# Latent attention: one run of value products per unit, with the denominators and the turned maxima inside it, and nine buffers of probabilities

## The chip, the core and the metric

The program runs on one core of one Trainium2 chip. The metric is the device time of one execution in microseconds (us); the time of a kernel is the median of its runs. A profile is one further execution, recorded instruction by instruction by the hardware profiler; its span is counted from the program's first recorded instruction to its last, so the execution's own time is a little longer than the span.

The engines are named as the profile names them: PE multiplies matrices (PEld is its weight load, which overlaps it), DVE works on vectors and can read the accumulator banks of PE (PSUM), ACT evaluates functions and copies, POOL works on vectors in SBUF, SP issues most DMA transfers. Each engine takes its instructions in order.

## The reference

Two layers over 256 context tokens and 1,024 latent tokens of width 1,024: a windowed attention layer, then a latent attention layer, each with modulation, gate and residual, and a final norm. Only the second layer's attention is touched. Cut to that:

```python
qn, qr, kn, kr, v, g = project(h)        # 16 heads; 64 + 32 columns of q and k, 64 of v
s = (einsum("bqhd,bkhd->bhqk", qn, kn)
     + einsum("bqhd,bkd->bhqk", qr, kr)) * scale
p = softmax(s, axis=-1)                  # over 256 + 1024 keys
o = einsum("bhqk,bkhd->bqhd", p, v)
y = (o * silu(g)) @ w_out
```

All is float32, and results are needed for the 1,024 latent queries alone.

## The kernel before

Latent attention is cut into 16 units (class `UnitB`, list `units`). A unit is one pair of heads and one half (512) of the queries; unit `ui` has pair `ui // 2` and half `ui % 2`. Its keys are ten chunks of 128 (`NT = 10`). The order of every instruction in this stage is the order in which the program writes it down (`manual_schedule`), and each engine works through its own part of that order. `u` is the unit at work, `pu` the one before, `nu` and `nnu` the next two.

**Scores.** `score(c, i0, i1)` multiplies the terms `i0` to `i1` of chunk `c`: five terms, each with one matmul per head of the pair (64 rows of the array each, line 1344), into a pair of PSUM banks. Pairs (3, 4) and (5, 6) alternate with `c % 2`; the last unit uses three pairs. After the fifth term ACT takes the exponential of both banks into one of six probability buffers `Er` (line 1348), and POOL adds the buffer to the running sum `acc` from which the denominators come (lines 1352 and 1354; on DVE in the last unit).

**Maxima of the next unit.** An upper bound for the row maximum is found a unit ahead: `nu.top(PIECES[c])` multiplies one piece of `nu`'s queries with keys into two of the banks 0, 1, 2 (line 1310), and DVE reduces each bank (lines 1316 and 1318). `CUT[c]` says after how many terms of chunk `c` this piece stands: 4, 1, 1, 2, 2, 3, 3, 4, 4, 5. At the unit's end `nu.turn` reduces the parts (line 1321) and turns the maxima with four matmuls (line 1324); `nu.shift` writes them with DVE into the rows of `nu.q` that the fifth score term reads (line 1328). So the fifth term of `nu`'s first chunk waits for the shift.

**Values.** `PV(c0, c1)` multiplies chunks of probabilities with the values into bank 7 (line 1361; each float32 product shows as two matmul instructions, so a chunk is four). There are two runs per unit: `PV(0, 5)` ahead of the scores of chunk 5, and `PV(5, NT)` after the last chunk. `fin` copies bank 7 out with ACT (line 1365) and loads the gate rows.

**Denominators.** Ahead of the first run stands `pu.fin2`: four matmuls with ones sum `pu`'s `acc` over its partitions (line 1372), ACT copies them into the first half of `acc` (line 1374). DVE inverts the two halves: `inv(0)` after the first run's place, `inv(1)` at the unit's end between `turn` and `shift` (line 1378). `gate` multiplies `pu`'s output by gate and inverse on POOL (line 1383) and stores it; it stands at chunk 0 of the unit after (`units[ui - 2].gate()`).

**Between units.** After the shift some units hold extra work ("fill"): units 0, 2, 4, 6, 8, 10 and 12 compute the keys of the next pair (`make_K`, three blocks, each copied out by ACT and DVE), units 3, 7 and 11 the values of the next four heads (`make_V`, five blocks, copied out by ACT). Units 1, 5, 9, 13 and 14 have none. Fill uses banks 0, 1, 2 as `top` does. `nnu.prep()` loads the queries of the unit after next into the buffer that the present unit's scores have just been reading, so it can only be issued when the last score is done, and `nu.top` of the next unit reads it first. One piece of the output weights is loaded and split per unit (`wo_fill`, an ACT copy and a POOL subtraction).

The arena `F` (52 KB per partition) holds the probability buffers from 10 KB on, the values from 34, the two `acc` from 44.

Of the kernel before, what the change touches and what calls it, by code (L numbers as in the profile page):

```python
# [22 lines left out]
NT = TOK // 128  # L23
# [1 line left out]
EPS = 1e-6  # L25
KB = 256
R_KB = 152
F_KB = 52
NEG = -1e30
A_SCALE = 64 ** -0.5  # L30
B_SCALE = 96 ** -0.5
# [2 lines left out]
class Ring:  # L34
# [6 lines left out]
    def next(self):  # L41
        b = self.bufs[self.i % len(self.bufs)]
        self.i += 1
        return b


def shp(ap, *dims):
    n = 1
    for d in dims:
        n *= d  # L50
    ap = ap[:, 0:n]
    if len(dims) == 1:
        return ap
    names = "abcdefg"[: len(dims)]
    kw = {c: d for c, d in zip(names[1:], dims[1:])}
    return ap.rearrange("p (" + " ".join(names) + ") -> p " + " ".join(names), **kw)
# [3 lines left out]
def kernel(ctx: ExitStack, tc: tile.TileContext, t, out, dbg=None):  # L60
    nc = tc.nc
# [4 lines left out]
    PB = ppool.tile([128, 8, 512], F32, name="PB")  # L66
    R = cpool.tile([128, R_KB * KB], F32R, name="arena_r")
    F = cpool.tile([128, F_KB * KB], F32, name="arena_f")
    ident = cpool.tile([128, 128], F32, name="ident")
# [16 lines left out]
    def r_at(kb, *dims):  # L86
        n = int(np.prod(dims))
        return shp(R[:, int(kb * KB) : int(kb * KB) + n], *dims)

    def f_at(kb, *dims):  # L90
        n = int(np.prod(dims))
        return shp(F[:, int(kb * KB) : int(kb * KB) + n], *dims)
# [395 lines left out]
    class UnitA:  # L488
# [29 lines left out]
        def score(self, h, later=False):  # L518
            g, qT = self.g, self.qT
            P = Pr.next()  # L520
            q = qT[:, h % 2, h // 2]
            self.Ps.append(P)
            sk = nsink[:, 4 * g + h : 4 * g + h + 1]
            nl = self.nloc * 128
            parts = [(nl, 256, 0, 0)]
            if nl:
                parts.append((0, nl, self.k0 * 128, (self.k0 - (self.ti - 1)) * 128))
            mx = None
            nm = self.nm[:, h : h + 1]
            for i, (po, n, ko, mo) in enumerate(parts):  # L530
                S = pss3()[:, 0:n]
                nc.tensor.matmul(S, q[:, 0], kT[:, g, ko : ko + n], start=True, stop=False)  # L532
                nc.tensor.matmul(S, q[:, 1], kT[:, g, ko : ko + n], start=False, stop=True)  # L533
                prev = sk if mx is None else mx
                mx = nm if i == len(parts) - 1 else self.mx[:, h : h + 1]
                o, mk = P[:, po : po + n], mask[:, mo : mo + n]
                if i == 0:
                    mk = zeros
                nc.vector.tensor_tensor_reduce(o, S, mk, -A_SCALE, prev, ALU.add, ALU.min, mx)  # L539
            if not later:  # L540
                self.exp(h)

        def exp(self, h):
            P, nm = self.Ps[h][:, 0 : self.nk], self.nm[:, h : h + 1]
            nc.scalar.activation(P, P, AF.Exp, bias=nm, scale=-1.0, accum_out=self.den[:, h : h + 1])  # L545
# [40 lines left out]
        def fin2(self, fast=False):  # L586
            g, og = self.g, self.og
            o, o2 = self.o, self.o2
            rt = shp(pst3(), 4, 128)
            for j in range(2):  # L590
                nc.tensor.transpose(rt[:, j, :], self.rb[:, j * 128 : j * 128 + 128], ident)
            rs = shp(rtr.next(), 2, 128)
            eng = nc.vector if fast else nc.gpsimd
            eng.tensor_add(o, o, o2)
            nc.vector.tensor_mul(rs, rt[:, 0:2, :], self.gt)
            eng.tensor_mul(o, o, rs)
            hi = og[:, 0, 2 * g : 2 * g + 2, :]
            eng.tensor_copy(hi, o)
            eng.tensor_sub(og[:, 1, 2 * g : 2 * g + 2, :], o, hi.bitcast(F32))
# [103 lines left out]
    def bank(g):  # L703
        return shp(PB[:, g % 4, :], 2, 256)
# [208 lines left out]
    for ui, u in enumerate(units):  # L913
# [9 lines left out]
        nu = units[ui + 1] if ui + 1 < len(units) else None  # L923
# [287 lines left out]
    NU = 16  # L1211
# [1 line left out]
    kTb = [r_at(o, 2, TOK) for o in (0, 10)]  # L1213
    KR = r_at(20, 2, TOK)
    qbufs = [r_at(o, 4, 512) for o in (10, 48, 32, 40)]
    Er = Ring(F, [10 + 4 * c for c in range(6)], 1024)
    accr = Ring(F, [44, 48], 1024)
    otr = Ring(F, [0, 2], 512)
    glr = Ring(R, [30, 112, 150], 512)
    KEYB = ((0, 512), (512, 512), (1024, 256))  # L1220
    PIECES = [[(0, 0)], [(0, 1)], [(1, 0)], [(1, 1)], [(0, 2), (1, 2)]]
    CUT = (4, 1, 1, 2, 2, 3, 3, 4, 4, 5)
    PIECES += [[(b + 2, i) for b, i in p] for p in PIECES]
    flat = krF.rearrange("p a b -> p (a b)")
    mxr = [flat[:, 128 * i : 128 * i + 128] for i in range(2)]
# [4 lines left out]
    topb = Banks(0, 1, 2)  # L1230
    psd = PB[:, 5, :]
# [49 lines left out]
    class UnitB:  # L1281
# [51 lines left out]
        def score(self, c, i0=0, i1=5):  # L1333


            q, kt = self.q, self.kt
            cs = slice(c * 128, c * 128 + 128)
            b = (5, 3, 0)[c % 3] if self.i == NU - 1 else 3 + 2 * (c % 2)
            terms = ((kt, 0, 0, 64), (kt, 0, 1, 64), (kt, 1, 0, 64), (KR, 0, 2, 64), (KR, 1, 3, 36))
            for i in range(i0, i1):  # L1340
                k, s, sq, n = terms[i]
                for e in range(2):
                    r = slice(64 * e, 64 * e + n)
                    nc.tensor.matmul(PB[:, b + e, :], k[r, s, cs], q[r, sq], start=i == 0, stop=i == 4)  # L1344
            if i0 == i1 or i1 < 5:
                return
            E = self.E[c] = shp(Er.next(), 2, 512)
            nc.scalar.activation(E, PB[:, b : b + 2, :], AF.Exp)  # L1348
            acc = shp(self.acc, 2, 512)
            eng = nc.vector if self.i == NU - 1 else nc.gpsimd  # L1350
            if c == 1:
                eng.tensor_add(acc, self.E[0], E)
            elif c:
                eng.tensor_add(acc, acc, E)  # L1354
# [14 lines left out]
        def fin2(self, bank):  # L1369
            acc = shp(self.acc, 2, 512)  # L1370
            for e, r in enumerate(HALF):
                nc.tensor.matmul(bank[r, :], ones, acc[:, e], start=True, stop=True)  # L1372
            self.rec = self.acc[:, 0:512]
            nc.scalar.copy(self.rec, bank)

        def inv(self, j):
# [35 lines left out]
    def fetch_out(ti):  # L1412
        o = shp(ogl.next(), 8, 128)
        load(out=o.bitcast(F32), in_=og_d[:, :, ti * 128 : ti * 128 + 128].rearrange("c p n -> p c n"))
        x = xr1.next().bitcast(F32)
        load(out=x, in_=x1_d[256 + ti * 128 : 384 + ti * 128, :])
        return o, x

    def cut_out(f):
        o, x = f  # L1420
        og = shp(ogr1.next(), 2, 8, 128)
        for h in range(2):
            hs = slice(4 * h, 4 * h + 4)
            split(og[:, 0, hs], og[:, 1, hs], o[:, hs].bitcast(F32))
        return og, x
# [81 lines left out]
    for ui, u in enumerate(units):  # L1507
        pu = units[ui - 1] if ui else None
        nu = units[ui + 1] if ui + 1 < NU else None
        nnu = units[ui + 2] if ui + 2 < NU else None  # L1510
        for c in range(NT):
            if c == 5:
                if pu:
                    pu.fin2(psd if nu else PB[:, 2, :])
                u.PV(0, 5)
                if pu:
                    pu.inv(0)
                if pu and nu is None:
                    pu.gate(0, 256)
                    first = fetch_out(0)  # L1520
                    pu.inv(1)
                    pu.gate(256, 512)
                    got = fetch_out(1)
            u.score(c, 0, CUT[c])
            if nu:
                nu.top(PIECES[c])
            if c == 0 and ui > 1:
                units[ui - 2].gate()
            u.score(c, CUT[c], 5)
            if 0 < ui < 12 and c == 2 or ui == 6 and c == 7 or ui in (12, 13) and c in (2, 7):  # L1530
                next(wo_fill, None)
            if nu is None and c == 0:
                load(out=gx1, in_=gate_d[1, 0, :].partition_broadcast(128))
                load(out=fg, in_=t["final_g"].partition_broadcast(128))
        if nnu:
            nnu.prep()
        u.PV(5, NT)
        if nu:
            filled = u.half == 0 and u.pair < 7 or ui % 4 == 3
            nu.turn(psd if filled else topb())  # L1540
            if pu:
                pu.inv(1)
            nu.shift()
            fillb.i = topb.i
            fill = make_K(u.pair + 1) if u.half == 0 and u.pair < 7 else iter(())
            if ui % 4 == 3:
                fill = make_V(ui // 4 + 1)
            for _ in fill:
                pass
        else:  # L1550
            ready = cut_out(first)
        u.fin()
# [81 lines left out]
```

## Time and profile before

| | |
|---|---|
| median of 3 runs | 1572.75 us (1570.41 to 1574.72) |
| the profiled execution's own time | 1573.23 us |
| its span | 1571.1 us |
| mean granted PE clock | 0.991 |
| span until the attention units of layer 2 begin, about | 1000 us |
| latent attention, first exponential of unit 0 to first of unit 15 | 1000.85 to 1455.97 us |
| last unit | 1455.97 to about 1477 us |
| output projection and final norm | to 1571.1 us |

The page of a profile counts instructions of each engine and their busy time, follows the chain of work that ended last, and groups instructions by line. A row of a group reads: line, engine, operation, output<-inputs, shapes, count | busy time in us, mean ns of one | idle time of the engine just ahead of them and what ended it. The view of waits adds up idle time by who waited for whom (total us, times, longest). In a timeline a row is a start, a duration and an instruction or a few equal ones; in brackets stands the idle time before it and what ended it. The windows view gives busy time of each engine in stretches of the span, with the PE clock that was granted.

### The profile page before, as it was taken

The page shows a single profiled execution, that of the slowest core. Times are in us where ns is not written, and L with a number is a line of the kernel's source. Part 1 is how long each engine was busy: PE and PEld are TensorE (multiplying, and loading weights), DVE is VectorE, ACT ScalarE, POOL GpSimd, SP SyncE. Part 2 cuts the span into 40 slices and gives each one's busy share as a digit, 9 for nine tenths or more (in the row PEclk, how much of TensorE's full clock was granted, in tenths as well). Part 3 has the DMA queues.
Part 4 walks back from the last instruction along what each step waited for, and adds up shares of the span by engine and source line. Part 5 has one row for each costly group of instructions (what it writes and reads, how often), then busy time and mean ns, then how long its engine had stood idle before and what let it go on. Part 6 is the DMA issues. An engine that isn't in the chain of part 4 may idle for free.

```text
span 1571.1 us, 24822 instructions
## 1 busy us (share of the span) xinstructions
PE 1522.2 (97%) x9074; PEld 1189.3 (76%) x9074; DVE 955.5 (61%) x1859; ACT 716.0 (46%) x1369; POOL 814.6 (52%) x764
## 2 busy tenths in 40 slices
PE   6899999998999999998999999999999999999998
PEld 2797888787888888887987888766766766766687
DVE  2666968827767778777726202566466566566644
ACT  2512112238777777777523422334444444444422
POOL 2652545326554343444318340378788789689300
PEclk8899999999999999999999999999999999999999
DMA  8425544574333333317204941402122112211442
GB/s 308 171 100 186 197 139 164 164 227 127 104 112 95 98 95 95 95 55 230 86 20 141 313 129 51 124 1 58 44 65 75 44 44 75 58 44 45 135 161 81
DMA packets 123985, 178.90 MB, mean 114 GB/s; under 512 B 11724, under 2 KB 72268, under 8 KB 123864
## 3 DMA queue, kind: packets, MB, share of 16 engines
q1 hardware_dynamic: 119032, 170.27, 34.0%
q10 hardware_dynamic: 4832, 7.06, 1.3%
q8 instruction: 71, 1.16, 0.3%
q14 instruction: 50, 0.41, 0.1%
HBM read 131.13 MB, written 46.15 MB: 113 GB/s over the span
## 4 chain that ended last, share of the span: by engine, by line
PE 83%; DVE 5%; DMA 3%; POOL 3%; issue 3%; ACT 3%; SPq 0%; POOLq 0%; DVEq 0%; ACTq 0%
PE PB L126 13%; PE PB L127 13%; PE PB L128 13%; PE PB L1344 12%; PE PB L1361 9%; PE PB L572 5%; PE PB L1310 5%; PE PB L562 4%; PE PB L532 2%; PE PB L533 2%; DMA arena_f<-a_w_in 1%; PE PB L1372 1%; DVE arena_f L344 1%; POOL arena_f L1103 1%; DVE arena_f L202 1%
## 5 line engine op out<-in xcount | busy, mean ns | idle before, releaser
L126 PE MATMUL PB<-arena_r 128*128 128x512 f32 (+2 forms) x1312 | 476.0, 363 | 4.1 <-ACT arena_r L205 2.1
L127 PE MATMUL PB<-arena_r 128*128 128x512 f32 (+2 forms) x1312 | 469.1, 358 | 2.8 <-POOL arena_r L729 1.9
L128 PE MATMUL PB<-arena_r 128*128 128x512 f32 (+2 forms) x1312 | 468.9, 358 | 0.2 <-DVE arena_r L122 0.2
L1354 POOL TENSOR_TENSOR arena_f<-arena_f 128x1024 f32<-128x1024 f32 x120 | 285.7, 2381 | 24.5 <-ACT arena_f L1348 17.6
L126 PEld LDWEIGHTS PB<-arena_r 128*128 128x128 f32 x1312 | 249.6, 190 | 50.6 <-issue 8.8
L127 PEld LDWEIGHTS PB<-arena_r 128*128 128x128 f32 x1312 | 249.5, 190 | 37.4 <-POOL arena_r L729 2.5
L128 PEld LDWEIGHTS PB<-arena_r 128*128 128x128 f32 x1312 | 249.4, 190 | 35.5 <-DVE arena_r L122 0.4
L1316 DVE TENSOR_REDUCE krF<-PB 128x1 f32<-128x512 f32 (+1 forms) x264 | 167.2, 678 | 124.7 <-PE PB L1310 124.7
L1348 ACT ACTIVATE arena_f<-PB 128x1024 f32<-128x1024 f32 x160 | 164.4, 1027 | 171.4 <-PE PB L1344 167.3
L1344 PE MATMUL PB<-arena_r 64*128 64x512 f32 (+1 forms) x1600 | 230.6, 396 | 0.2 <-DVE arena_r L1328 0.2
L122 POOL TENSOR_TENSOR arena_r<-arena_f,arena_r 128x512 fp32r<-128x512 f32 x98 | 134.1, 1381 | 161.6 <-ACT arena_r L121 160.2
L1344 PEld LDWEIGHTS PB<-arena_r 64*128 64x128 f32 (+1 forms) x1600 | 166.5, 185 | 37.6 <-issue 14.2
L122 DVE TENSOR_TENSOR arena_r<-PB,arena_r 128x512 fp32r<-128x512 f32 (+2 forms) x215 | 140.4, 664 | 82.7 <-ACT arena_r L121 81.8
L539 DVE CUSTOM_DVE_ANT_0 arena_f<-PB,arena_f,small 128x256 f32<-128x256 f32 (+1 forms) x288 | 145.5, 524 | 46.9 <-PE PB L533 40.3
L121 ACT CAST arena_r<-PB 128x512 fp32r<-128x512 f32 (+2 forms) x215 | 120.4, 565 | 99.5 <-PE PB L128 52.1
L1361 PE MATMUL PB<-arena_f 128*64 128x512 f32 x640 | 143.6, 595 | 0.0
L545 ACT ACTIVATE arena_f<-arena_f,small 128x640 f32<-128x640 f32 (+2 forms) x160 | 118.9, 744 | 28.8 <-DVE small L539 27.7
L572 PE MATMUL PB<-arena_r 128*128 128x512 f32 x336 | 120.7, 435 | 4.3 <-ACT arena_f L583 4.1
L344 DVE SCALAR_TENSOR_TENSOR arena_f<-arena_f,small 128x512 f32<-128x512 f32 x98 | 114.3, 1211 | 10.6 <-DMA arena_f<-ada_w 10.2
L1310 PE MATMUL PB<-arena_r 64*128 64x512 f32 (+1 forms) x768 | 117.3, 357 | 2.2 <-DVE arena_r L122 0.7
L1361 PEld LDWEIGHTS PB<-arena_f 128*64 128x64 f32 x640 | 44.4, 137 | 84.5 <-issue 81.8
L562 PE MATMUL PB<-ident,arena_f 128*128 128x128 f32 x672 | 105.3, 273 | 0.4 <-ACT arena_f L545 0.3
(165 smaller groups left out, 1868.4 us busy)
## 6 DMA issues: line engine op xcount, KB each, us to landing
arena_r<-q_d SPq DMA_DIRECT2D x160, 128.0 KB, 2.9
arena_f<-ada_w SPq DMA_DIRECT2D x64, 256.0 KB, 3.0
arena_f<-a_w_in SPq DMA_DIRECT2D x40, 256.0 KB, 3.6
arena_f<-ada_w SPq DMA_DIRECT2D x16, 512.0 KB, 5.0
arena_f<-x SPq DMA_DIRECT2D x16, 512.0 KB, 5.7
q_d<-arena_f SPq DMA_DIRECT2D x16, 512.0 KB, 2.6
qn_d<-arena_f SPq DMA_DIRECT2D x16, 512.0 KB, 4.6
arena_r<-qn_d SPq DMA_DIRECT2D x16, 512.0 KB
```

The source lines that it names most:

```text
L122: (lo_eng or nc.vector).tensor_sub(lo, src, hi.bitcast(F32))
L126: nc.tensor.matmul(o, ah, bh, start=first, stop=False)
L127: nc.tensor.matmul(o, al, bh, start=False, stop=False)
L128: nc.tensor.matmul(o, ah, bl, start=False, stop=last)
L562: nc.tensor.transpose(pt[:, h, :], self.Ps[h][:, ci * 128 : ci * 128 + 128], ident)
L572: nc.tensor.matmul(self.pv, V[:, self.chunks[ci], self.g, :], PT[:, s], start=ci == 0 and s == 0, stop=ci == self.m - 1 and s == 1,)
L1310: nc.tensor.matmul(bank[:, o : o + n], self.q[r, s, bs], k[r, 0, n0 : n0 + n], start=s == 0, stop=s == 2)
L1316: nc.vector.reduce_max(self.mxp[:, e, b : b + 1, i], bank[:, 0:n], AX.X)
L1344: nc.tensor.matmul(PB[:, b + e, :], k[r, s, cs], q[r, sq], start=i == 0, stop=i == 4)
L1348: nc.scalar.activation(E, PB[:, b : b + 2, :], AF.Exp)
L1354: eng.tensor_add(acc, acc, E)
L1361: nc.tensor.matmul(PB[r, 7, :], Vq[:, c, h, :], E[:, e], start=c == 0, stop=c == NT - 1)
```

## The change

The probability ring grows from six buffers to nine, a buffer `recb` of its own takes the denominators, `CUT` becomes 3 for every chunk, and in units 0 to 14 the value products stand in one run after the last score. In this run stand, in PE's order: chunk 0; `pu`'s denominators; chunks 1 to 4; the turn of `nu`'s maxima; chunks 5 to 9. The exponential of the last chunk is written down after the product of chunk 0, since it takes chunk 0's buffer. The two banks of chunk 8's scores take the denominators and the turned maxima; bank pairs alternate with `c + i`, so the next unit's chunk 0 uses the pair of chunk 9. `shift` now stands ahead of both halves of `inv`. The last unit keeps its two runs. The arena grows by 14 KB per partition, and the reserve for DMA descriptors in SBUF is set to 1,024 bytes.

```diff
-F_KB = 52
+F_KB = 66
...
-    Er = Ring(F, [10 + 4 * c for c in range(6)], 1024)
+    Er = Ring(F, [10 + 4 * c for c in range(6)] + [52, 56, 60], 1024)
+    recb = f_at(64, 512)
...
-    CUT = (4, 1, 1, 2, 2, 3, 3, 4, 4, 5)
+    CUT = 3
...
-            b = (5, 3, 0)[c % 3] if self.i == NU - 1 else 3 + 2 * (c % 2)
+            b = self.bank(c)
...
-            if i0 == i1 or i1 < 5:
-                return
+            if i1 == 5 and (c < NT - 1 or self.i == NU - 1):
+                self.exp(c)
+
+        def bank(self, c):
+            return (5, 3, 0)[c % 3] if self.i == NU - 1 else 3 + 2 * ((c + self.i) % 2)
+
+        def exp(self, c):
+            b = self.bank(c)
             E = self.E[c] = shp(Er.next(), 2, 512)
...
-            self.rec = self.acc[:, 0:512]
+            self.rec = recb if self.i < NU - 1 else self.acc[:, 0:512]
...
-            if c == 5:
-                if pu:
-                    pu.fin2(psd if nu else PB[:, 2, :])
+            if c == 5 and nu is None:
+                pu.fin2(PB[:, 2, :])
                 u.PV(0, 5)
...
-            u.score(c, 0, CUT[c])
+            u.score(c, 0, CUT)
             if nu:
                 nu.top(PIECES[c])
...
-            u.score(c, CUT[c], 5)
+            u.score(c, CUT, 5)
...
         if nnu:
             nnu.prep()
-        u.PV(5, NT)
+        if nu is None:
+            u.PV(5, NT)
+        else:
+            b = u.bank(NT - 2)
+            u.PV(0, 1)
+            u.exp(NT - 1)
+            if pu:
+                pu.fin2(PB[:, b, :])
+            u.PV(1, 5)
+            nu.turn(PB[:, b + 1, :])
+            nu.shift()
+            if pu:
+                pu.inv(0)
+                pu.inv(1)
+            u.PV(5, NT)
         if nu:
-            filled = u.half == 0 and u.pair < 7 or ui % 4 == 3
-            nu.turn(psd if filled else topb())
-            if pu:
-                pu.inv(1)
-            nu.shift()
             fillb.i = topb.i
...
-    nc = bacc.Bacc("TRN2", target_bir_lowering=False, num_devices=1)
+    nc = bacc.Bacc("TRN2", target_bir_lowering=False, num_devices=1, dynamic_dma_scratch_size=1024)
```

More of the change, by code (lines that the diff above doesn't have):

```diff
@@ L1511 @@
         for c in range(NT):
-            if c == 5:
-                if pu:
-                    pu.fin2(psd if nu else PB[:, 2, :])
+            if c == 5 and nu is None:
+                pu.fin2(PB[:, 2, :])
                 u.PV(0, 5)
-                if pu:
[L1517 to L1520, printed above, removed]
-                    pu.inv(1)
-                    pu.gate(256, 512)
-                    got = fetch_out(1)
-            u.score(c, 0, CUT[c])
+                pu.inv(0)
+                pu.gate(0, 256)
+                first = fetch_out(0)
+                pu.inv(1)
+                pu.gate(256, 512)
+                got = fetch_out(1)
+            u.score(c, 0, CUT)
             if nu:
@@ L1536 @@
             nnu.prep()
-        u.PV(5, NT)
-        if nu:
-            filled = u.half == 0 and u.pair < 7 or ui % 4 == 3
-            nu.turn(psd if filled else topb())
-            if pu:
-                pu.inv(1)
-            nu.shift()
+        if nu is None:
[10 more added lines that the diff above has]
+            if pu:
+                pu.inv(0)
+                pu.inv(1)
+            u.PV(5, NT)
+        if nu:
             fillb.i = topb.i
```

## The prediction

> **What bounds the kernel now.** I read the page first, for the span, the chain that ended last and the costliest groups.
>
> ```profile
> span 1571.1 us, 24822 instructions
> PE 1522.2 (97%) x9074; PEld 1189.3 (76%) x9074; DVE 955.5 (61%) x1859; ACT 716.0 (46%) x1369; POOL 814.6 (52%) x764
> ...
> PE 83%; DVE 5%; DMA 3%; POOL 3%; issue 3%; ACT 3%; SPq 0%; POOLq 0%; DVEq 0%; ACTq 0%
> PE PB L126 13%; PE PB L127 13%; PE PB L128 13%; PE PB L1344 12%; PE PB L1361 9%; PE PB L572 5%; PE PB L1310 5%; PE PB L562 4%; PE PB L532 2%; PE PB L533 2%; DMA arena_f<-a_w_in 1%; PE PB L1372 1%; DVE arena_f L344 1%; POOL arena_f L1103 1%; DVE arena_f L202 1%
> ...
> L1354 POOL TENSOR_TENSOR arena_f<-arena_f 128x1024 f32<-128x1024 f32 x120 | 285.7, 2381 | 24.5 <-ACT arena_f L1348 17.6
> ```
>
> PE sets the end. The change lies in lines 1310 to 1383, so I asked for windows of units 0 to 14 (first exponential of unit 0 to first of unit 15) and of unit 14, which has no fill.
>
> ```profile
> 1000.85:1455.97 455.12, 453.41 (x3241) 306.18 (x3242) 275.99 (x394) 197.67 (x232) 373.60 (x177) 1.00 0.19 55
> 1428.80:1455.97 27.17, 26.93 (x196) 17.36 (x196) 17.37 (x25) 11.44 (x12) 25.12 (x12) 1.00 0.07 21
> ```
>
> The columns are the length, then PE, PEld, DVE, ACT and POOL busy, the granted clock (1.00: nothing to lose or win there), DMA. PE looks busy for 453.4 of 455.1 us. That hides what can be won, since a matmul that starts late overlaps its neighbours. The start times show it. These are ACT's exponentials of unit 14 (line 1348), from ACT's timeline:
>
> ```profile
> 1428.80 1.03 ACT L1348 ACTIVATE arena_f<-PB 128x1024 f32<-128x1024 f32 x1 [1.69 <-PE PB L1344]
> 1430.83 1.03 ACT L1348 ACTIVATE arena_f<-PB 128x1024 f32<-128x1024 f32 x1 [1.00 <-PE PB L1344]
> ...
> 1435.69 1.03 ACT L1348 ACTIVATE arena_f<-PB 128x1024 f32<-128x1024 f32 x1 [0.62 <-PE PB L1344]
> ...
> 1442.81 1.03 ACT L1348 ACTIVATE arena_f<-PB 128x1024 f32<-128x1024 f32 x1 [5.52 <-PE PB L1344]
> 1444.43 1.03 ACT L1348 ACTIVATE arena_f<-PB 128x1024 f32<-128x1024 f32 x1 [0.59 <-PE PB L1344]
> 1446.05 1.03 ACT L1348 ACTIVATE arena_f<-PB 128x1024 f32<-128x1024 f32 x1 [0.58 <-PE PB L1344]
> ```
>
> A chunk undisturbed takes 1.62 us (1442.81 to 1444.43 to 1446.05). Two intervals are longer: chunk 0 to chunk 1 takes 2.03, and chunk 4 to chunk 5, with the first run between, 7.12. The chain of waits of the same stretch (start, us, what) tells why:
>
> ```profile
> 1426.48 0.22 PE PB L1324 x4
> 1426.70 1.12 PE PB L1344 x8
> 1427.82 0.50 PE PB L1310 x4
> 1428.32 0.69 DVE krF L1316
> ...
> 1435.59 1.01 PE PB L1372 x4
> 1436.60 4.29 PE PB L1361 x20
> 1440.89 0.90 PE PB L1344 x6
> ...
> 1453.91 0.68 DVE arena_r L1328
> ...
> 1454.63 0.71 DVE arena_r L1328
> ```
>
> **The change, part by part.** All savings are PE start times.
>
> *One run instead of two.* Chunk 4 to chunk 5 holds one chunk (1.62) and 24 matmuls. Twenty take 4.29 us, so 24 take 5.15. 7.12 - 1.62 - 5.15 leaves 0.35 us: the price of going from 64-row score matmuls to 64-column ones and back. The denominators (line 1372) and the turn (1324) stand beside a run now and inside one afterwards, so nothing is added. One change of kind, in and out, goes per unit: 15 x 0.35 = 5.3 us. Bounds: 0, if the 0.35 belongs to the first product of a run wherever it stands and not to the change of kind, and 6.3 (0.42 each). The run's other entry and exit remain.
>
> *CUT = 3.* Before, chunk 0's piece stands after four terms and chunk 1's after one, so two `top`s come within 2 terms and one piece. The second needs a bank that DVE is still reducing. The waits of units 0 to 14 (total us, times, longest) carry it:
>
> ```profile
> PEld PB L1310 <- DVE krF L1316: 7.7, 15, 0.6
> PEld PB L1310 <- DMA arena_r<-qr_d: 0.6, 1, 0.6
> PEld PB L1344 <- DVE arena_r L1328: 0.5, 1, 0.5
> PEld PB L1372 <- POOL arena_f L1352: 0.4, 1, 0.4
> ...
> POOL arena_f L1352 <- ACT arena_f L1348: 88.0, 14, 35.3
> POOL arena_f L1354 <- ACT arena_f L1348: 17.6, 15, 1.4
> ```
>
> It falls once in each unit. On the spacing of exponentials it is worth 2.03 - 1.62 = 0.41 us in unit 14, and in unit 9 (after a key fill) 2.18 - 1.62 = 0.56:
>
> ```profile
> 1278.06 1.02 ACT L1348 ACTIVATE arena_f<-PB 128x1024 f32<-128x1024 f32 x1 [1.03 <-PE PB L1344]
> 1280.24 1.03 ACT L1348 ACTIVATE arena_f<-PB 128x1024 f32<-128x1024 f32 x1 [1.15 <-PE PB L1344]
> ```
>
> With CUT at 3 pieces come every 1.62 us; a pair of reductions takes 1.29 to 1.36, so DVE keeps up from the first piece, with little to spare (0.3 us a chunk). I take 0.45 for each of 15 units, 6.8 us; bounds 0 and 7.7.
>
> *The loads of the queries.* `prep` is released by the last score, and the next unit's first `top` reads it. Before, only the second run lies between. In unit 5 that is too short:
>
> ```profile
> 1175.99 0.42 SPq L1300 DMA_DIRECT2D arena_r<-qr_d  x1
> ...
> 1180.94 0.51 PEld L1310 LDWEIGHTS PB<-arena_r 64*128 64x128 f32 x2 [0.62 <-DMA arena_r<-qr_d]
> ```
>
> Afterwards the whole run (44 matmuls, 9.4 us at 0.2145) lies between. The same six DMAs stand on SP with nothing moved past them; the stall goes, with a little lateness in unit 9: 0.8 us, bounds 0.6 and 1.0.
>
> *Turn and shift inside the run.* Before, the fifth term of the next first chunk follows the shift closely; at the border to the last unit, which has no `top` to fill the time, the wait shows (0.5 us in the list, and in the chain as two DVE steps). Afterwards five chunks (4.29 us) cover the shift: -0.5 us. The turn itself now stands in front of 20 value matmuls and waits for DVE's last reductions; these end, as now, about 2.2 us after the start of the last `top`, and the turn comes at least 5 us after it. If DVE were later than that, PE would stop for the difference, once a unit.
>
> *Both reciprocals behind the shift.* DVE's durations:
>
> ```profile
> L1378 DVE RECIPROCAL arena_f<-arena_f x32: 1695/1744/1754, 1039.4 to 1479.4; 128x256 f32<-128x256 f32 x32
> ...
> L1328 DVE TENSOR_TENSOR arena_r<-PB,ident x32: 683/690/698, 997.2 to 1454.6; 4x512 fp32r<-4x512 f32 x32
> ```
>
> From the turn on DVE needs 2 x 0.69 + 2 x 1.74 = 4.9 us. It is wanted next by the first piece of the next unit: 4.29 for the products, then by the chain above 1.12 + 0.50 less two of eight score matmuls (0.23), at 5.7 us. So 0.8 us is spare without a fill, 3 us and more with one, where key splits stand behind the reciprocals on DVE. Cost 0; if the cover were gone, PE would stop by DVE's lateness in four units without fill (unit 14's successor has no `top`).
>
> *Nine buffers, last exponential held back.* It now waits for chunk 0's product (0.86 us) and takes 1.03; its own product stands 9 chunks, over 8 us, later. Cost 0. Behind it on ACT stands the copy of the denominators, awaited by the reciprocals alone, which come 3 us later. Exponentials now bunch in the first 16 us of a unit, while POOL needs 2.4 + 8 x 2.38 = 21.4 us for the sums. POOL's idle time ahead of them is 88.0 - 35.3 (the wait for unit 0 left out) + 17.6 = 70 us, near 4.7 per unit of 30.3; a unit shorter by 0.9 leaves 3.8, and nine buffers take the lag. Cost 0.
>
> *`recb`.* The wait of 0.4 us for POOL in the last unit's denominators goes, since unit 14's sums start earlier: -0.4, bounds 0 and 0.5. New banks are free: chunk 8's exponential is a chunk old. The smaller descriptor reserve costs nothing if the loads here don't use it; the issues listed by the page are SP's and ACT's, none is POOL's.
>
> *Sum:* 5.3 + 6.8 + 0.8 + 0.5 + 0.4 = 13.8 us. The profiled execution's own time is 1573.23 (2.1 around its span), so 1559.4. It stood 0.5 above the median of the runs, 1572.75: forecast **1559.0 us**.
>
> **The rivals.**
> - *The change of kind is not what costs 0.35.* Then the second entry is repaid elsewhere: 1559.0 + 5.3 = 1564.3 us. For it: the row is an interval, no single wait. Against: inside a run the matmuls keep their pace, and denominators to products already join without a seam (1435.59 + 1.01 = 1436.60).
> - *The gap at chunk 1 stays,* since both reciprocals now stand right ahead of the first pieces and DVE has only 0.3 us a chunk to catch up: 1559.0 + 6.8 = 1565.8 us. Against: the 0.8 us spare above.
> - *Slower: reciprocals wait for POOL's adds.* The place is the pair behind the shift. If each had to wait out an add under way, up to 2.38 us, DVE would be free at 4.9 + 4.8 = 9.7 us after the turn and 4.0 late for the first piece in four units: 16 us. With a key fill (3.7 us) the three splits stand behind it and the first `top` gets its second bank some 2.2 us late, 7 times: 15 us. Together 1559.0 + 31 = 1590 us. It outweighs the gain from about 1.7 us of waiting for each reciprocal. Against: 32 reciprocals took 1695 to 1754 ns with POOL busy for 373.6 of 455.1 us, so a wait of that kind would have shown.
>   The Trainium skill ("SBUF — State Buffer", section "SBUF: two separate sides") says that VectorE and GpSimd take a shared pair of ports as an exclusive lock, the loser blocking for the whole instruction, when the VectorE operation runs in a mode with two ports or has two SBUF inputs. Were the reciprocal such an operation, that rule would give this rival; the narrow spread of the row speaks against it.
> - *Nothing to be seen:* the first two together, 1559.0 + 12.1 = 1571.1 us; a reserve that does slow loads would lead there as well.
>
> **How the numbers follow.** About 0.3%, 4.7 us, is what a measurement of this kernel can tell from no change; that puts the border at 1568.0. Forecast 0.72, the first and second rival 0.09 each, the slower one 0.04, nothing to be seen 0.06. The low end takes the upper bounds (6.3 + 7.7 + 1.0 + 0.7 + 0.5 = 16.2, to 1556.6) and a microsecond and a half for the runs' own spread: 1555. The high end, 1567, takes in the first two rivals. Faster holds the forecast but for 0.03 of it, and both first rivals: 0.87; same 0.08, with part of the slower rival at a short wait; slower 0.05.
>
> **What would show it.** Right: exponentials of chunks 0 to 8 evenly 1.62 us apart in every unit; 44 value and denominator matmuls and the turn in one unbroken stretch of about 9.7 us; units without fill near 26.3 us instead of 27.2; no wait of line 1310 for DVE or DMA. Wrong: a wait of PE for the turn or for DVE at the first piece (the second rival; with longer or delayed reciprocals the third); idle ACT ahead of an exponential released by POOL; a run of 44 that is longer than 9.7 us (the first rival). A difference ahead of 1000 us would mean that something outside these steps moved.

## The result, and the profile after

| | before | changed |
|---|---|---|
| median | 1574.35 us (6 runs, 1570.41 to 1575.09) | 1562.31 us (6 runs, 1560.26 to 1563.35) |
| profiled execution, own time | 1573.23 us | 1563.35 us |
| span | 1571.1 us | 1561.6 us |
| units 0 to 14, first exponential of unit 0 to first of unit 15 | 455.12 us | 442.25 us |

The ratio is 0.9926, 95% interval 0.9914 to 0.9939: 12.0 us faster between the medians. The forecast was 1559.0 with 1555 to 1567.

Windows view of the changed kernel, units 0 to 14 and unit 14 (columns as before: length, PE, PEld, DVE, ACT and POOL busy, clock, DMA):

```profile
1003.20:1445.45 442.25, 442.25 (x3240) 321.83 (x3238) 275.13 (x393) 196.35 (x232) 374.73 (x178) 1.00 0.20 57
1419.55:1445.45 25.90, 25.90 (x196) 16.87 (x194) 17.26 (x25) 11.35 (x12) 25.20 (x13) 1.00 0.08 22
```

PE is now busy for the whole stretch, where 1.7 us were left before; the other 11 us gained were hidden inside "busy". The stretch lost 12.87 us. ACT's timeline of unit 14, chunks 0 to 9, then unit 15's first exponential:

```profile
1419.55 1.03 ACT L1355 ACTIVATE arena_f<-PB 128x1024 f32<-128x1024 f32 x1 [1.31 <-PE PB L1345]
1421.13 1.03 ACT L1355 ACTIVATE arena_f<-PB 128x1024 f32<-128x1024 f32 x1 [0.55 <-PE PB L1345]
...
1424.37 1.03 ACT L1355 ACTIVATE arena_f<-PB 128x1024 f32<-128x1024 f32 x1 [0.58 <-PE PB L1345]
1426.02 1.03 ACT L1355 ACTIVATE arena_f<-PB 128x1024 f32<-128x1024 f32 x1 [0.61 <-PE PB L1345]
1427.65 1.03 ACT L1355 ACTIVATE arena_f<-PB 128x1024 f32<-128x1024 f32 x1 [0.61 <-PE PB L1345]
...
1432.59 1.03 ACT L1355 ACTIVATE arena_f<-PB 128x1024 f32<-128x1024 f32 x1 [0.62 <-PE PB L1345]
1435.27 1.03 ACT L1355 ACTIVATE arena_f<-PB 128x1024 f32<-128x1024 f32 x1 [1.65 <-PE PB L1368]
...
1445.45 1.03 ACT L1355 ACTIVATE arena_f<-PB 128x1024 f32<-128x1024 f32 x1 [0.85 <-PE PB L1345]
```

Chunk 0 to chunk 1 takes 1.58 us, not 2.03. The last exponential is released by line 1368, the product of chunk 0, as written. One thing is not as forecast: from chunk 4 on a chunk takes (1432.59 - 1426.02) / 4 = 1.64 us, not 1.62. The chain of waits shows a run, after unit 13:

```profile
1407.79 1.01 PE PB L1368 x4
1408.80 0.86 PE PB L1379 x4
1409.66 3.43 PE PB L1368 x16
1413.10 0.22 PE PB L1325 x4
1413.31 4.29 PE PB L1368 x20
1417.60 0.90 PE PB L1345 x6
1418.50 0.45 PE PB L1311 x2
1418.96 1.16 PE PB L1345 x10
```

Denominators and turn sit in it without a seam; from 1407.79 to 1417.60 it takes 9.81 us. The forecast named a run longer than 9.7 us as a sign of its first rival, but its 9.7 counts the 44 matmuls and the turn at the pace inside a run and leaves out the entry into it, which stays. The first four products take 1.01 us, where the four denominators inside the run take 0.86: 0.15 more. The six score matmuls behind the run take 0.90; at the pace of the ten that follow (1.16) they would take 0.70: 0.20 more. These two together are the 0.35 us that the forecast read from the interval, and they now stand once in a unit. Units without fill take 26.38 us, and unit 14 25.90, where the forecast had 26.3.

The list of waits of the stretch names no wait of line 1311 (the pieces) for DVE or for a load any more. POOL's idle time ahead of its sums, without the wait for unit 0, is 90.5 - 34.7 = 55.8 us, 3.7 a unit, as forecast (3.8); before it was 70:

```profile
POOL arena_f L1359 <- ACT arena_f L1355: 90.5, 14, 34.7
...
PEld PB L1345 <- issue: 4.4, 6, 0.8
PEld PB L1345 <- ACT arena_f L1355: 0.3, 1, 0.3
```

In this one profile unit 0 begins 2.35 us later than before (1003.20 against 1000.85), after the same instructions on every engine, and 1.0 us more passes from the start of the last matmul to the end (7.71 against 6.71, the landing of the last store). It is the slowest execution of its six; the last experiments come back to it.

### The profile page after: what moved, and what is told of

The parts are those of the page before. It is cut to its first block, busy times and chain, and to the rows that moved or that the text cites. A ratio compares the mean times of both kernels' runs of the same rounds, so it can differ in the third digit from the quotient of the medians.

```text
span 1561.6 us, 24793 instructions
## 1 busy us (share of the span) xinstructions
PE 1513.9 (97%) x9074; PEld 1207.1 (77%) x9074; DVE 953.2 (61%) x1859; ACT 714.1 (46%) x1369; POOL 816.3 (52%) x764
## 3 DMA queue, kind: packets, MB, share of 16 engines
q8 instruction: 71, 1.16, 0.3%
## 4 chain that ended last, share of the span: by engine, by line
PE 86%; DMA 3%; DVE 3%; ACT 3%; issue 2%; POOL 2%; SPq 0%; POOLq 0%; DVEq 0%; ACTq 0%
PE PB L126 14%; PE PB L127 14%; PE PB L128 14%; PE PB L1345 12%; PE PB L1368 9%; PE PB L572 5%; PE PB L1311 5%; PE PB L562 4%; PE PB L532 2%; PE PB L533 2%; DMA arena_f<-a_w_in 1%; PE PB L1379 1%; DVE arena_f L344 1%; DMA arena_f<-b_w_in 1%; PE PB L355 1%
## 5 line engine op out<-in xcount | busy, mean ns | idle before, releaser
L1345 PE MATMUL PB<-arena_r 64*128 64x512 f32 (+1 forms) x1600 | 225.8, 395 | 0.0
L1345 PEld LDWEIGHTS PB<-arena_r 64*128 64x128 f32 (+1 forms) x1600 | 174.0, 185 | 17.2 <-issue 5.2
L1311 PE MATMUL PB<-arena_r 64*128 64x512 f32 (+1 forms) x768 | 109.5, 354 | 0.7 <-DVE arena_r L122 0.7
```

What stands on the lines that cost most here:

```text
L1311: nc.tensor.matmul(bank[:, o : o + n], self.q[r, s, bs], k[r, 0, n0 : n0 + n], start=s == 0, stop=s == 2)
```

## The experiments

The measure that tells most is the stretch named above, read from one profile of each kernel. Two profiles of the changed kernel gave 442.25 and 442.22 us, two of one variant 440.63 and 440.73, and the kernel before 455.12 and, with another reserve, 455.18; so 0.2 us can be told there, while medians tell about a microsecond.

### The positions of the pieces, alone and undone

```diff
-    CUT = (4, 1, 1, 2, 2, 3, 3, 4, 4, 5)
+    CUT = (3,) * 10
```

> The kernel before with CUT 3 for every chunk and nothing else. My theory: the gap between the exponentials of chunk 0 and chunk 1 comes from two top pieces standing too close. It then goes here as well: chunk 0 to chunk 1 takes 1.6 us in place of 2.0 to 2.2, the stretch from the first exponential of unit 0 to that of unit 15 falls from 455.1 to about 448 us, the time by 7 us. Rival: the gap comes from DVE being held by the shift and the reciprocals at the unit's border, which stay where they were. Then it stays at 2.0 us or more and the stretch at 455.

Measured: 1567.36 us, ratio to the kernel before 0.9961 (0.9946 to 0.9976). Windows view, then ACT's timeline of unit 14:

```profile
1001.51:1450.45 448.94, 448.48 (x3241) 312.54 (x3239) 275.82 (x393) 197.75 (x232) 373.56 (x177) 1.00 0.19 56
```
```profile
1423.69 1.03 ACT L1348 ACTIVATE arena_f<-PB 128x1024 f32<-128x1024 f32 x1 [1.73 <-PE PB L1344]
1425.31 1.03 ACT L1348 ACTIVATE arena_f<-PB 128x1024 f32<-128x1024 f32 x1 [0.58 <-PE PB L1344]
```

The gap is gone (1.62 us) with shift and reciprocals where they were. The stretch lost 6.2 us.

The other way round, the changed kernel with the old positions:

```diff
-    CUT = 3
+    CUT = (4, 1, 1, 2, 2, 3, 3, 4, 4, 5)
...
-            u.score(c, 0, CUT)
+            u.score(c, 0, CUT[c])
...
-            u.score(c, CUT, 5)
+            u.score(c, CUT[c], 5)
```

> The changed kernel with the old positions of the pieces (4, 1, 1, 2, 2, 3, 3, 4, 4, 5). My theory: the gap at chunk 1 comes back, 0.45 to 0.55 us in each unit, the stretch is 449 us in place of 442.3, the time 7 us above the changed kernel. Rival (DVE was freed by the moved shift and reciprocals): 442.3, no change.

With 5 as the last position the last unit takes its last exponential, and that chunk's sum, twice; units 0 to 14 are whole. Measured: 1567.67 us, ratio 0.9959 (0.9947 to 0.9970), stretch 448.73, 6.5 us more than the changed kernel. The list of waits:

```profile
PEld PB L1311 <- DVE krF L1317: 8.0, 15, 0.6
```

The wait is back, once in each unit, although DVE does its shift and reciprocals early here. Both runs say the same: two pieces too close make it, not what DVE does at the border.

### Two runs instead of one

```diff
+            if c == 5 and nu:
+                if pu:
+                    pu.fin2(PB[:, u.bank(5), :])
+                u.PV(0, 5)
+                if pu:
+                    pu.inv(0)
             u.score(c, 0, CUT)
...
-            if i1 == 5 and (c < NT - 1 or self.i == NU - 1):
+            if i1 == 5:
...
-            u.PV(0, 1)
-            u.exp(NT - 1)
-            if pu:
-                pu.fin2(PB[:, b, :])
-            u.PV(1, 5)
+            u.PV(5, 7)
             nu.turn(PB[:, b + 1, :])
             nu.shift()
             if pu:
-                pu.inv(0)
                 pu.inv(1)
-            u.PV(5, NT)
+            u.PV(7, NT)
```

> The changed kernel with two runs per unit: denominators and chunks 0 to 4 ahead of chunk 5's scores, the first reciprocal there too, chunks 5 to 9 with the turn at the end; CUT 3, nine buffers, recb and the bank order stay. By the forecast's step a second change of kind costs 0.35 us a unit: stretch 442.3 + 5.2 = 447.5. My theory after the result: the pace of chunks after the two short pieces (256 columns) at chunk 4 is 1.645 us in place of 1.615 until a run of products sets the two streams of PE right again, so a run in the middle gives back about 0.03 x 4 a unit: 442.3 + 5.2 - 1.8 = 445.7, with chunks 5 to 8 1.62 apart. Rival (a run costs nothing by itself): 442.3.

Measured: 1566.70 us, ratio 0.9959 (0.9945 to 0.9973).

```profile
1001.89:1449.17 447.28, 447.18 (x3240) 311.02 (x3238) 277.10 (x393) 197.60 (x233) 372.54 (x177) 1.00 0.20 56
```
```profile
1429.50 1.02 ACT L1355 ACTIVATE arena_f<-PB 128x1024 f32<-128x1024 f32 x1 [0.61 <-PE PB L1345]
...
1436.62 1.03 ACT L1355 ACTIVATE arena_f<-PB 128x1024 f32<-128x1024 f32 x1 [5.52 <-PE PB L1345]
```

The stretch is 5.0 us longer than with one run, and chunk 4 to chunk 5 in unit 14 is again 7.12 us. That total is near the 5.2 that the forecast's step gives, but not for its reason alone. By units, ten of 15 are 0.23 to 0.29 us longer, so a second run costs a net 0.25, the 0.35 less what chunks 5 to 8 gain by the better pace after it (they are 1.62 us apart on the mean of the units, as expected). That is 3.8 us in all. The rest, 1.2 us, is in single units: units 9 and 13, which have no fill, are 0.65 and 0.78 us longer instead of 0.25, three others 0.32 to 0.44. Here the loads of the queries again have only half a run to land in, and the list of waits has one such wait, at the end of unit 13:

```profile
PEld PB L1311 <- DMA arena_r<-qr_d: 0.5, 1, 0.5
```

For unit 9 the list has none, though in the chain of waits the first piece behind that run takes 0.70 us, where it takes 0.45 with one run. That a load holds it there, and makes the three others longer, is likely but not shown. My expectation of 445.7 left these waits out.

### The pace after the short pieces

The pieces of the fourth key block are 256 columns wide; two of them share a chunk, 4 and 9 in the changed kernel. Here they move to 8 and 9:

```diff
     PIECES += [[(b + 2, i) for b, i in p] for p in PIECES]
+    PIECES = [p for p in PIECES if len(p) == 1] + [p for p in PIECES if len(p) == 2]
```

> The changed kernel with the two pairs of short pieces (256 columns) moved from chunks 4 and 9 to chunks 8 and 9; the other pieces move up. My theory: the slower pace (1.645 us a chunk) starts with the first short pieces, so chunks 4 to 7 now take 1.615 and the stretch falls by 0.03 x 4 x 15 = 1.8 us to 440.5. Rival: the pace depends on how far the unit is (more engines at work later), the chunks stay at 1.645 from chunk 4 on and the stretch at 442.3.

Measured: 1559.22 us, ratio 0.9909 (0.9889 to 0.9930), stretch 440.63. ACT's timeline of unit 14:

```profile
1416.40 1.03 ACT L1356 ACTIVATE arena_f<-PB 128x1024 f32<-128x1024 f32 x1 [1.31 <-PE PB L1346]
...
1422.84 1.03 ACT L1356 ACTIVATE arena_f<-PB 128x1024 f32<-128x1024 f32 x1 [0.59 <-PE PB L1346]
...
1427.68 1.03 ACT L1356 ACTIVATE arena_f<-PB 128x1024 f32<-128x1024 f32 x1 [0.59 <-PE PB L1346]
1429.33 1.03 ACT L1356 ACTIVATE arena_f<-PB 128x1024 f32<-128x1024 f32 x1 [0.62 <-PE PB L1346]
```

Chunks 4 to 7 now take (1427.68 - 1422.84) / 3 = 1.61 us, and chunk 8, behind the first short pieces, 1.65. The slower pace goes with the short pieces and not with the time in the unit.

A second look at the same question, the changed kernel with the piece of chunk 4 one term earlier:

```diff
-    CUT = 3
+    CUT = (3, 3, 3, 3, 2, 3, 3, 3, 3, 3)
```

> The changed kernel with the piece of chunk 4 (the first pair of short pieces) after two terms in place of three. With the old positions, where chunk 4 had it after two terms as well, chunks 4 to 7 kept 1.61 us. If the place of the short pieces among the terms sets the pace, chunks 4 to 7 take 1.61 to 1.62 and the stretch is 440.5, as with the short pieces moved to the end. Rival (the growing positions of the later chunks did it): 1.645 from chunk 5 on and 442.3.

Measured: 1561.54 us, ratio 0.9919 (0.9904 to 0.9933), stretch 442.07.

```profile
1420.12 1.03 ACT L1355 ACTIVATE arena_f<-PB 128x1024 f32<-128x1024 f32 x1 [0.62 <-PE PB L1345]
1421.86 1.03 ACT L1355 ACTIVATE arena_f<-PB 128x1024 f32<-128x1024 f32 x1 [0.71 <-PE PB L1345]
1423.47 1.03 ACT L1355 ACTIVATE arena_f<-PB 128x1024 f32<-128x1024 f32 x1 [0.59 <-POOL arena_f L1361]
...
1428.31 1.03 ACT L1355 ACTIVATE arena_f<-PB 128x1024 f32<-128x1024 f32 x1 [0.59 <-PE PB L1345]
```

Half a hit. Chunks 4 to 8 keep (1428.31 - 1421.86) / 4 = 1.61 us, so the place of the short pieces among the terms does set the pace. But chunk 3 to chunk 4 now takes 1.74, and the stretch gains 0.2 us at most, the least that can be told, of the 1.8 expected. In the kernel with all the old positions, where the pieces of chunks 3 and 4 both stand after two terms, chunk 3 to chunk 4 of unit 14 takes 1.64 and the next chunks 1.61; so the 1.74 goes with two pieces that stand one term closer. What in PE makes the pace is not settled.

### What DVE has to spare behind the shift

```diff
                 pu.inv(0)
                 pu.inv(1)
+                for _ in range(2):
+                    nc.vector.reciprocal(pu.rec[:, 0:128], pu.rec[:, 0:128])
             u.PV(5, NT)
```

> The changed kernel with two more reciprocals of 128 columns each behind the pair (the second undoes the first), so about 1.75 us more of DVE work between shift and the next unit's first reductions. The forecast gave DVE 0.8 us to spare there in units without fill and over 3 us in the others. If so, DVE is 0.9 us late after units 1, 5, 9 and 13: chunk 0 to chunk 1 takes up to 0.9 us longer in the unit after these four and nowhere else, the stretch from the first exponential of unit 0 to that of unit 15 rises by up to 3.8 us, from 442.3 to about 445.5. Rival (DVE has much more to spare): 442.3, no wait of line 1311 for DVE. Second rival (none to spare): all units longer, by 1.75 us in those without fill.

Measured: 1563.92 us, ratio 0.9933 (0.9919 to 0.9948), stretch 446.12, 3.9 us more than the changed kernel. The units after 1, 5, 9 and 13 need 2.54, 2.55, 2.56 and 2.52 us from chunk 0 to chunk 1, all others 1.39 to 1.63. DVE's timeline after unit 13, and the list of waits:

```profile
1414.27 1.41 DVE L1329 TENSOR_TENSOR arena_r<-PB,ident 4x512 fp32r<-4x512 f32 x2 [4.68 <-PE PB L1325]
1415.72 3.37 DVE L1385 RECIPROCAL arena_f<-arena_f 128x256 f32<-128x256 f32 x2
1419.00 1.89 DVE L1556 RECIPROCAL arena_f<-arena_f 128x128 f32<-128x128 f32 x2
1420.91 2.58 DVE L1317 TENSOR_REDUCE krF<-PB 128x1 f32<-128x512 f32 x4
```
```profile
PEld PB L1311 <- DVE krF L1317: 3.6, 4, 0.9
```

The addition took 1.89 us, and 0.94 of it reached PE (2.54 against 1.60): DVE has about 0.95 us to spare where the forecast had 0.8, and at least the whole 1.89 with a fill.

### The turn at the end of the run

```diff
             if pu:
                 pu.fin2(PB[:, b, :])
-            u.PV(1, 5)
-            nu.turn(PB[:, b + 1, :])
-            nu.shift()
             if pu:
                 pu.inv(0)
                 pu.inv(1)
-            u.PV(5, NT)
+            u.PV(1, NT)
+            nu.turn(PB[:, b + 1, :])
+            nu.shift()
```

> The changed kernel with the reciprocals ahead of the turn and the turn and the shift behind all ten chunks of products. My theory: with CUT 3 the fifth term of the next chunk 0 comes about 1.8 us after the turn's start and the shift ends 1.7 us after it, so units with and without fill keep their length; only unit 14, whose successor has no top pieces, waits 0.4 to 0.5 us. Stretch 442.3 + 0.5 = 442.8. Rival (the turn inside the run is what keeps PE from waiting at every border without fill): 0.35 us and more in units 1, 5, 9, 13, 14, stretch 444 or more.

Measured: 1562.05 us, ratio 0.9926 (0.9911 to 0.9941), stretch 443.50. The chain at the end of unit 14:

```profile
1441.75 0.24 PE PB L1325 x4
...
1442.73 0.71 DVE arena_r L1329
1443.44 0.04 issue
1443.48 2.57 PE PB L1345 x18
```

The expectation lies between the two outcomes: +1.3 us, not 0.5 and not 1.75. Units with a fill keep their length, units 1, 5, 9 and 13 are 0.16 us longer, unit 14 is 0.65 longer, since PE there waits for the shift. Having the turn inside the run is worth that 1.3 us.

### The reserve, and the time outside the stretch

```diff
-    nc = bacc.Bacc("TRN2", target_bir_lowering=False, num_devices=1)
+    nc = bacc.Bacc("TRN2", target_bir_lowering=False, num_devices=1, dynamic_dma_scratch_size=1024)
```

> The kernel before with the reserve for DMA descriptors at 1,024 bytes and nothing else. My theory: loads and stores don't use it; time as before within 0.3%, stretch 455.1. Rival: it slows loads, which the part ahead of the attention units and the last store would show (unit 0's first exponential at 1003 us and the last store 1 us later, as in the profile of the changed kernel).

Measured: 1573.84 us, ratio 1.0003 (0.9994 to 1.0013), stretch 455.18, unit 0 at 1001.54 us, 6.71 us from the start of the last matmul to the end. The reserve costs nothing.

The changed kernel, and the one with late short pieces, once more side by side:

> The changed kernel once more, beside the version with late short pieces on the same chip, with a second profile. My theory: the extra 2.3 us ahead of unit 0 and 1.0 us behind the last matmul in its first profile are the spread of single executions; here unit 0's first exponential falls between 999 and 1003 us, the stretch is again 442.3 within 0.2, the median near 1562. Rival: the extra time belongs to the kernel and comes again.

> The changed kernel with the short pieces in chunks 8 and 9, once more, against the changed kernel on the same chip. By the stretch (440.6 against 442.3) it is 1.6 us faster, near 1560.5 us; rival: the 3 us between the two medians so far are real, so 1559.

Measured: the changed kernel 1561.24 us (5 runs), ratio 0.9919 (0.9907 to 0.9932), stretch 442.22; with late short pieces 1560.09 us, ratio 0.9905 (0.9890 to 0.9921), stretch 440.73. Windows view of the one, then of the other:

```profile
1002.85:1445.07 442.22, 442.22 (x3240) 322.39 (x3238) 275.15 (x393) 196.31 (x232) 374.57 (x178) 1.00 0.20 57
```
```profile
1001.81:1442.54 440.73, 440.73 (x3240) 321.56 (x3238) 275.17 (x393) 196.42 (x233) 374.22 (x178) 1.00 0.20 57
```

The stretch repeats to 0.1 us. The second profile of the changed kernel is again of its longest execution (1563.11 of 1560.40 to 1563.11), with unit 0 at 1002.85 us and 7.85 us from the start of the last matmul to the end. Over all profiles here the first number lies between 999.10 and 1003.20 us, in no order by kernel. The second is 6.70 to 6.71 in the three profiles with the old arena; of the nine with the larger arena two have 6.70 and 6.71 and seven have 7.00 to 7.85. So the extra time at the end came again in the changed kernel, as the rival said, and goes with the kernels of the larger arena, though not in each. Which part of the change would make it was not found, and this stays open. Between the medians 12.0 and 12.9 us are gained, against 12.87 in the stretch, which leaves no more than 1 us for it.

The version with late short pieces has the shortest stretch and the lowest medians of all: 1.5 and 1.6 us less than the changed kernel in the stretch, in both profiles, and 1559.22 and 1560.09 us against 1562.31 and 1561.24. The medians alone could not tell so little.

## Why the prediction was right

The direction, the place and the likeliest case were right: 12.0 us of the 13.8 forecast. The forecast time was 3.3 us too low; 1.6 of it is the kernel before, whose median was 1574.35 in these runs and not 1572.75. The experiments lie on a path, before, CUT alone, CUT with everything but the single run, the changed kernel, so the stretch can be split by subtraction:

| step of the forecast | forecast, us | stretch, us | runs |
|---|---|---|---|
| CUT = 3 | 6.8 | 6.2 | 455.12 to 448.94; undone 6.5 |
| loads of the queries, turn and shift | 0.8 + 0.5 | 1.7 | 448.94 to 447.28 |
| one run instead of two | 5.3 | 5.0 | 447.28 to 442.25 |
| POOL's wait | 0.4 | 0 | from unit 15's first exponential to the start of the last matmul 108.4 us in both |
| sum | 13.8 | 12.9 | |

The second row also holds the nine buffers, `recb` and the order of banks, which were not run alone. How rows two and three share the waits for loads depends on the path, since these waits move: they stand in unit 5 in the kernel before and with CUT alone, in unit 13 with two runs.

*One run instead of two:* its size was right by luck, by two errors that cancel. The price of changing the kind of matmul is there as read, 0.35 us a run (7.12 again with two runs), but the forecast took an undisturbed chunk as 1.62 us throughout. That row was read from chunks 5 to 7 of the kernel before, right behind a run. Without a run at chunk 5 the chunks behind the short pieces take 1.64, and about 0.1 us a unit goes there: net 0.25, 3.8 us. The other 1.2 us are in single units of the kernel with two runs; a wait for a load is listed for one of them, and for the rest it is argued. This is the mis-sized term: 5.3 forecast, 3.8 measured. The first rival (the price stays) fell with the two-run kernel.

*Turn and shift:* the forecast counted 0.5 us, at the border to the last unit alone. The kernel with the turn at the end shows 0.65 there and 0.16 in each of units 1, 5, 9 and 13, for which the forecast had nothing: 1.3 us together. What these four wait for is open.

*CUT = 3:* right in mechanism, shown from both sides. It was counted at 0.45 a unit; the gap itself closed by more (chunk 0 to chunk 1 fell from 2.09 to 1.58 on the mean of 15 units, in the kernel with CUT alone too, 7.8 us in sum). There chunks 1 to 7 took 0.9 us back and the borders 0.7, so 6.2 were left. The second rival, that the gap stays, fell: no wait for DVE is left.

*Both reciprocals behind the shift:* 0.8 us to spare was forecast, and the added reciprocals found 0.95. The slower rival, reciprocals that wait for POOL's adds, has no trace:

```profile
L1385 DVE RECIPROCAL arena_f<-arena_f x32: 1694/1720/1754, 1054.0 to 1468.9; 128x256 f32<-128x256 f32 x32
```

They take what they took before (1695/1744/1754), with POOL busy 374.7 of 442.3 us; in the trace 28 of the 32 begin while an operation of POOL is running. No run here made a DVE operation wait for POOL at that place, so the rule on the shared ports in the Trainium skill ("SBUF — State Buffer", section "SBUF: two separate sides") is not refuted; it only does not show for these reciprocals.

*POOL's wait:* the forecast put it in the last unit, but the list ends where that unit begins, and the timeline of the kernel before has the wait in unit 14, ahead of unit 13's denominators:

```profile
1434.72 0.87 PE L1344 MATMUL PB<-arena_r 64*128 64x512 f32 x5
...
1435.52 0.20 PEld L1372 LDWEIGHTS PB<-arena_f,small 128*64 128x64 f32 x4 [0.37 <-POOL arena_f L1352]
1435.52 1.08 PE L1372 MATMUL PB<-arena_f,small 128*64 128x512 f32 x4
```

It was idle time of the weight load while PE was still at the score matmuls (to 1435.59). Chunk 4 to chunk 5 takes 7.12 us in unit 14, as in the units without this wait, so there was nothing to gain. Here idle time of PEld cost PE nothing; only the timeline of PE tells that.

*Nine buffers, held exponential, banks, reserve:* cost 0, as forecast; no wait of PE in the list names them beyond one of 0.3 us.

## What to carry to other kernels

When an engine shows 99% busy and its instructions overlap, read start-to-start times of a regular consumer (here the exponentials) against the undisturbed interval; that found 13 us, 11 of which busy time hid. Take the undisturbed interval from the place where the work will stand after the change, not from the best stretch of the old kernel. Two uses of a small set of buffers that stand unevenly cost more than the same two spaced evenly, and that can be tried by itself before anything else is rebuilt.

## What the runs showed of the hardware that was not expected

When a pair of 256-column pieces (line 1311) stands behind the third term of a chunk, the chunks that follow take 1.64 us in place of 1.61 until the next run of products; with the pairs moved to chunks 8 and 9, chunks 4 to 7 keep 1.61, and so they do with the first pair behind the second term. The count of matmuls and the granted clock (1.00) are the same. The distance in time between the two heads' score matmuls does not tell the two paces apart. In unit 9 of the changed kernel it stays at 50 ns from chunk 4 on and in unit 14 at 16 to 17 ns, but in units 5 and 13 it drifts all the while, and chunks 5 to 7 take 1.64 to 1.65 us in all four. What makes the slower pace is open.
